# A two-layer attention trunk: k scaled by ScalarE in mixer B's prologue, later root steps, other steps for the weight splits, k stacks placed inside the v products, and a reordered start

## The chip, the cores and the metric

The kernel runs on one core of a Trainium2 chip. The metric is the device time of one execution in microseconds (us); the median of several runs is given. Engines are called as in the profile: PE (TensorE), DVE (VectorE), ACT (ScalarE), POOL (GpSimd), SP (SyncE, which here only issues DMAs). PE, DVE, ACT and POOL each carry out their own instructions in the order of the program and meet through semaphores; an instruction that waits holds up all that stand behind it on its engine.

## The reference

1024 tokens of width 1024 go through two layers. Layer 0 uses mixer A, neighbourhood attention over a 16 x 64 token grid: each query sees 8 x 16 keys around it, with a learned bias. Layer 1 uses mixer B, attention with 16 query heads and 4 key/value heads of 64; q and k are normalised per head and rotated by their grid position:

```python
proj = h @ w_in
q, k, v, gate = jnp.split(proj, [MIX_WIDTH, MIX_WIDTH + kv_w, MIX_WIDTH + 2 * kv_w], axis=-1)
q = rms_norm(q..., q_norm_g); k = rms_norm(k..., k_norm_g)
q = _apply_axial_rope(q, tabs); k = _apply_axial_rope(k, tabs)
sc = jnp.einsum('bkgqd,bksd->bkgqs', qb, k) * scale
pr = jax.nn.softmax(sc, axis=-1)
o = jnp.einsum('bkgqs,bksd->bkgqd', pr, v)
return (o * jax.nn.silu(gate)) @ w_out
```

Ahead of each mixer stands an RMS norm over the 1024 columns, behind it a residual sum and a gated projection of a per-layer embedding (in the kernel `ple`, `pp`). A last RMS norm ends the trunk.

## The kernel before

**Products.** Each float32 product is made of three products in a rounded form (fp32r): high by high, high by low and low by high, where the low half of a value is what its rounding left. So every operand of PE exists twice, as `HTh` and `HTl` (the normed tokens, transposed), `wh` and `wl` (weights), `PTh` and `PTl` (transposed attention weights), `KA` and `KB` (keys). `mm` (L324) is one matmul, `split3` three. A high half is a copy on ACT (a PSUM or SBUF source, an fp32r target), a low half a subtraction, mostly on DVE.

**Weights.** The class `Weights` (`WQ`) keeps the order in which 128 x 1024 units of weights are used. `stage` loads a unit by SP's DMA (L216) into one of two `wstage` buffers; a unit's load can start when the unit two before it is split, so SP's queue waits there, with the DMAs behind it. `pump` splits the next loaded unit: the high half at once (ACT, L235), the low half (L240) at the next `settle`, on DVE in one operation of 1024 columns or on POOL in four of 256 (`WQ.low`). `gate` says whether `pump` may split: `False` no, `True` one split and then `False`, `None` always. `get` forces whatever the product at hand still lacks. A split unit's staging buffer is free after its low half.

**Order.** `pulse()` runs `WQ.pump` and `post.tick`; what was put off by `post.add(n, f)` runs n pulses later. `mix(att, dense)` interleaves two lists: it runs the items of `att` one by one, a pulse behind each, and dense items in between in proportion to their written costs.

**Start of mixer A** (L942 to L1047), an order written out by hand: for token tile t, `load` (SP), `square` and `root` (ACT), `newton` (DVE, from tile 3 on `newton_p` on POOL), `scale` (DVE L923, whole or by halves of 512 columns), `ht` (four transposes L506 by PE, `HTh` L507 by ACT, `HTl` L508 by DVE, per half). `vpart(t, a, b)` runs items a to b of tile t's v products; chunk i of them uses unit i of the weights `avv`, and for tiles 0 and 1 a chunk comes in three items, one for each kind of product (the last of a chunk's three may be the one with `wl`). `split()` forces one split, both halves. The first unit's low half is on DVE, the following on POOL.

**Mixer B** has a prologue and 128 steps. The prologue makes q, k, v of the first heads (`qkv_items`, products of 512 columns into the one `d` bank), and half of the second heads'. Behind each fourth token tile `finish_norm` takes the norms of four tiles, 24 values each row: in the prologue (`pro[0]`) Newton steps on DVE, then `scale_tile` (L1229 to L1232) multiplies k tiles (128 x 128, two heads) on DVE and q tiles (128 x 256, four heads) on POOL. Later it is a `power` on POOL (L1217), a root step `newton` of three DVE operations (L1220 to L1222), and the scalings on POOL one pulse apart; a norm of more than 16 values (the second heads' q and k, two such norms) has four pulses more between them. `k_stack(i, hf)` transposes four k tiles (PE L1271, into `psT`, a pool of two banks) and makes `KA` (ACT) and `KB` (DVE, with copies on POOL) from them. `k_stack(1, ...)` makes keys that are first used near step 62.

Step n of 0 to 127 treats one head, half and tile: `f_S` (scores, PE; the minimum, DVE L1371), `f_E` (exponential, ACT L1377), `f_T` (8 transposes, PE L1389, in two banks of `psT`; `PTh` ACT L1391, `PTl` DVE L1392), and at even n `f_AV`, the product with v over two steps, first all matmuls with `PTh`, then what stands in `turned` (q stacks, transposes by PE into `psT`), then all with `PTl`. A step takes about 4.2 us. Step n's items of `att` are `turn`, [`f_AV`], `f_T` and `f_E` in either order, `f_S` of step n + 2, each with a pulse. The dense items between them are the second heads' qkv products (g = 0), gates, q products (g = 1, 2), and at the end `pp` (g = 3). `scores` sets `WQ.gate` to `True` behind odd n and to `False` behind even n below 112, and to `None` from 112 on; `turn` sets a `True` that wasn't used to `False`. So weights are split at one place in odd steps, and freely at the end.

Of the kernel before, what the change touches and what calls it, by code (L numbers as in the profile page):

```python
# [15 lines left out]
AF = mybir.ActivationFunctionType  # L16
# [17 lines left out]
DG, DR, DQ, DY, NP = 1, 2, 2, 1, 8  # L34
# [10 lines left out]
KD, KS = 3, 4  # L45
# [118 lines left out]
def trunk(ctx, tc, x, wts, rpb, gains, hgains, mask, sides, rope, gain0, out):  # L164
    nc = tc.nc
    sync, act, dve, pool, pe = nc.sync, nc.scalar, nc.vector, nc.gpsimd, nc.tensor
# [99 lines left out]
    WQ = Weights()  # L266
# [54 lines left out]
    post = Later()  # L321
# [180 lines left out]
    def to_ht(pt, t, xn, cs=(0, 1)):  # L502
        for c in cs:
            ps = pt.tile([128, 4, 128], F32, name="t")
            for k in range(4):
                pe.transpose(ps[:, k], xn[:, (4 * c + k) * 128:(4 * c + k + 1) * 128], ident)  # L506
            act.activation(HTh[:, t, 4 * c:4 * c + 4], ps, AF.Copy)  # L507
            dve.tensor_tensor(HTl[:, t, 4 * c:4 * c + 4], ps, HTh[:, t, 4 * c:4 * c + 4], ALU.subtract)  # L508
# [183 lines left out]
    def mixer_a():  # L692
        jobs = weight_sums()
        with ExitStack() as es:
# [195 lines left out]
            def load(t):  # L890
                sync.dma_start(X[t], x[t])

            def square(t):
                act.activation(junk, X[t], AF.Square, accum_out=stat[:, 0, t:t + 1])
# [4 lines left out]
            def newton(t):  # L899
                ss, y, r = stat[:, 0, t:t + 1], stat[:, 1, t:t + 1], stat[:, 2, t:t + 1]  # L900
                h, w = wk[:, 8 + t:9 + t], wk[:, 16 + t:17 + t]
                dve.tensor_scalar(h, ss, -0.5 / D, -0.5 * EPS, op0=ALU.mult, op1=ALU.add)  # L902
                dve.reciprocal(y, wk[:, t:t + 1])
                dve.scalar_tensor_tensor(w, y, h, y, op0=ALU.mult, op1=ALU.mult)
                dve.scalar_tensor_tensor(r, w, 1.5, y, op0=ALU.add, op1=ALU.mult)
# [15 lines left out]
            def scale(t, n=1024, cs=None):  # L921
                for c in cs or range(0, 1024, n):
                    dve.scalar_tensor_tensor(X[t][:, c:c + n], X[t][:, c:c + n], stat[:, 2, t:t + 1], gain[:, c:c + n],  # L923
                                             op0=ALU.mult, op1=ALU.mult)

            def ht(t, cs=(0, 1)):
                to_ht(psT, t, X[t], cs)
# [5 lines left out]
            def split():  # L933
                WQ.pump(True)
                WQ.settle()
# [21 lines left out]
            def vpart(t, a, b):  # L957
                for f in vs[t][a:b]:
                    f()
# [22 lines left out]
            root(2)  # L982
            scale(1, 512, (512,))
            newton(2)
            for t in range(5, NT - 1):
                load(t)
            X.append(ini.tile([128, D], F32, name="X", bufs=NT - 1))
            load(NT - 1)
            vpart(1, 0, 3)
            ht(1, (1,))  # L990
            scale(2, 512, (0,))
            vpart(1, 3, 5)
            vpart(0, 5, 6)
            vpart(1, 5, 6)
            ht(2, (0,))
            scale(2, 512, (512,))
            square(3)
            newton_p(3)
            split()
            vpart(2, 0, 1)  # L1000
            ht(2, (1,))
            split()
# [81 lines left out]
            for h in range(NH):  # L1084
                att = []
                for j in range(NT):
                    n = h * NT + j
# [28 lines left out]
                dense = []  # L1116
# [15 lines left out]
    def mixer_b(pend):  # L1132
        with ExitStack() as es:
# [30 lines left out]
            turned = []  # L1164
# [35 lines left out]
            def finish_norm(ss, tiles):  # L1200
                wk = sb.tile([128, 96], F32, name="wk", bufs=1)
                n = ss.shape[1]
                if pro[0]:
                    ops = [lambda: dve.tensor_scalar(ss, ss, 0.5 / HD, 0.5 * EPS, op0=ALU.mult, op1=ALU.add)]
                    ops += rsqrt_ops(ss, ss, wk)
                    for i in range(2):
                        post.add(1 + i, lambda i=i: [f() for f in ops[6 * i:6 * i + 6]])
                    for raw, rs in tiles:
                        post.add(2, lambda raw=raw, rs=rs: scale_tile(raw, rs, dve if rs.shape[1] == 2 else pool))
                    return  # L1210
                y, a = wk[:, 0:n], wk[:, n:2 * n]

                def power():
                    dve.tensor_scalar(ss, ss, 4.0 / HD, 4.0 * EPS, op0=ALU.mult, op1=ALU.add)
                    for c in range(0, n, 8):
                        w = slice(c, min(c + 8, n))
                        pool.tensor_tensor(y[:, w], ss[:, w], mhalf[:, :w.stop - c], ALU.pow)  # L1217

                def newton():
                    dve.tensor_tensor(a, y, y, ALU.mult)  # L1220
                    dve.scalar_tensor_tensor(a, a, -1.0, ss, op0=ALU.mult, op1=ALU.mult)
                    dve.scalar_tensor_tensor(ss, a, 3.0, y, op0=ALU.add, op1=ALU.mult)  # L1222
                post.add(DR, power)
                at = DR + NP + (4 if n > 16 else 0)
                post.add(at - 1, newton)
                for i, (raw, rs) in enumerate(tiles):
                    post.add(at + i, lambda raw=raw, rs=rs: scale_tile(raw, rs))

            def scale_tile(raw, rs, eng=pool):  # L1229
                nh = rs.shape[1]  # L1230
                r3 = raw.rearrange("p (h d) -> p h d", h=nh)
                eng.tensor_tensor(r3, r3, rs[:, :, None].to_broadcast([128, nh, 64]), ALU.mult)  # L1232

            def q_items(g, eng):
# [181 lines left out]
            def gates(p):  # L1416
                return [i for hf in range(2) for i in gate_items("bg", p, hf, dalloc, sb, gg)]

            def stacks(i):
                return [(lambda hf=hf: k_stack(i, hf), 450.0) for hf in range(2)]  # L1420
            first, second = qkv_items(0, dve, 4), qkv_items(1, pool, 2)
            ks, gf = stacks(0), gates(0)
# [13 lines left out]
            def exps(n):  # L1436
                def f():
                    f_E(*steps[n])
                f.first = True
                return f  # L1440

            def blocks(n):
                def f():
                    f_T(*steps[n])
                f.kind = "apart" if n % 2 else "blocks"
                return f
            for g in range(4):
                att = []
                for n in range(32 * g, 32 * g + 32):
                    h, hf, t = steps[n]  # L1450
                    av = n >= 2 and n % 2 == 0
                    w = CB if av else CN
                    def turn():
                        if WQ.gate:
                            WQ.gate = False
                        later.tick()
                    att.append((turn, w[0]))
                    if av:
                        att.append((lambda n=n: f_AV(*steps[n - 1]), w[1]))
                    te = [(blocks(n), w[2])]  # L1460
                    if n + 1 < len(steps):
                        te.append((exps(n + 1), w[3]))
                    if n % 2 == 0 and n > 0:
                        te.reverse()
                    att += te
                    if n + 2 < len(steps):
                        def scores(n=n):
                            f_S(*steps[n + 2])
                            WQ.gate = n % 2 == 1 if n < 112 else None
                        att.append((scores, w[4]))  # L1470
                    m = n + QS_AT
                    if m % 8 == 0 and m < len(steps):
                        hn, fn, _ = steps[m]
                        att.append((lambda hn=hn, fn=fn: turned.append(lambda: q_stack(hn // 2, fn)), 0.0))
                    if YLOAD_B <= n < YLOAD_B + NT:
                        att.append((lambda t=n - YLOAD_B: load_y(1, t), 0.0))
                if g == 3:
                    def last():
                        end[0] = 1
                        f_AV(*steps[-1])  # L1480
                    att.append((last, CB[1]))
                dense = []
                if g == 0:
                    gd = gates(1)
                    n = len(gd) // 2
                    dense += second[10:16] + gd[:n] + second[16:] + gd[n:]
                elif g == 3:
                    WQ.cap[3] = 2
                    dense += gates(6) + gates(7) + pp_items(1, dalloc, sb, TAGS_B)
                else:  # L1490
                    gd = gates(2 * g)
                    n = len(gd) // 2
                    qi = q_items(g + 1, pool)
                    ks = stacks(1) if g == 1 else []
                    dense += gd[:n] + ks[:1] + gd[n:] + qi[:KS] + ks[1:] + qi[KS:8] + gates(2 * g + 1) + qi[8:]
                mix(att, dense, hold=HOLD + 1 if g == 3 else 0)
            post.flush()
            later.flush()
# [466 lines left out]
```

## Time and profile before

| | us |
|---|---|
| median of 3 runs | 1500.2 (1499.02 to 1501.57) |
| the profiled execution | 1498.04 |
| its span, first to last instruction | 1496.3 |
| mean granted TensorE clock | 0.999 |
| DMA moved | 157.61 MB, 105 GB/s on the mean |

| from to (us) | part | PE busy |
|---|---|---|
| 0 to 50 | start of mixer A | 45.76 of 50 |
| 700 to 760 | prologue of mixer B | 58.48 of 60 |
| 760 to 890 | mixer B, first steps | 129.21 of 130 |
| 890 to 975 | steps with the moved parts | 80.53 of 85 |
| 975 to 1190 | | 215.00 of 215 |
| 1190 to 1320 | last steps of mixer B | 127.50 of 130 |

Lines of the timeline read: start, duration, engine, line of the program, operation, output tile and input tiles, shape, count (rows of the same kind that follow each other are joined, the duration is then from the first start to the last end), and in brackets how long the engine was idle before and whose end released it ("issue": nothing that the profile shows). Matmuls overlap in PE's pipe, so a matmul's duration is longer than the distance to the next start.

### The profile page before, as it was taken

Reading aid. Unit: us, or ns where it says so; the run is one execution under the profiler, and the core shown is the slowest. Engines: PE = TensorE matmul, PEld = TensorE weight load, DVE = VectorE, ACT = ScalarE, POOL = GpSimd, SP = SyncE. Lnnn points to the kernel's source line nnn. Section 1 sums busy time; section 2 is a strip of 40 time slices with the busy share of each in tenths; the row PEclk is TensorE's granted clock in tenths of the full one; section 3 lists DMA queues with packets and bytes.
Section 4 is the critical chain, followed back from the end, with each engine's and each line's share of the span. In section 5 each row is a group of like instructions: output and inputs, shape, how many; then the busy total and the mean of one; then the engine's idle time right before and its main releaser. Section 6 shows DMA issues by size and latency. Waiting matters only on the chain.

```text
span 1496.3 us, 23431 instructions
## 1 busy us (share of the span) xinstructions
PE 1473.0 (98%) x8305; PEld 1271.4 (85%) x8305; DVE 1057.6 (71%) x1922; ACT 910.5 (61%) x1820; POOL 469.0 (31%) x651
## 2 busy tenths in 40 slices
PE   8999999999999999999999999999999999999997
PEld 6888888988988887888878887889999988888886
DVE  4467776477477598757766787777877777789845
ACT  5477766477377535433456776767767777745432
POOL 3246775387265200020154352323140400000000
PEclk9999999999999999999999999999999999999999
DMA  6424574283132963262220111101101121763223
GB/s 225 134 89 152 108 164 138 65 171 97 36 89 85 332 245 99 93 207 85 71 71 12 40 51 45 35 23 42 59 28 44 57 64 64 247 238 107 79 97 128
DMA packets 91460, 157.61 MB, mean 105 GB/s; under 512 B 18256, under 2 KB 54352, under 8 KB 90832
## 3 DMA queue, kind: packets, MB, share of 16 engines
q1 hardware_dynamic: 87344, 143.80, 29.0%
q0 software_dynamic: 2560, 8.39, 3.9%
q10 hardware_dynamic: 1440, 3.94, 0.8%
q8 instruction: 66, 1.08, 0.3%
q14 instruction: 50, 0.41, 0.1%
HBM read 125.56 MB, written 50.83 MB: 118 GB/s over the span
## 4 chain that ended last, share of the span: by engine, by line
PE 53%; DVE 5%; ACT 2%; issue 1%; DMA 0%; POOL 0%; DVEq 0%; ACTq 0%; POOLq 0%
PE d L324 27%; PE s L324 9%; PE o L324 8%; PE t L1389 7%; PE t L506 1%; DVE PTl L1392 1%; PE t L324 1%; DVE wl L240 1%; ACT PTh L1391 0%; DVE mn L1371 0%; PE t L1341 0%; DVE xn L1742 0%; ACT wh L235 0%; DVE X L1631 0%; DVE QS L1351 0%
## 5 line engine op out<-in xcount | busy, mean ns | idle before, releaser
L324 PE MATMUL d<-wh,HTh 128*128 128x512 f32 (+1 forms) x800 | 285.3, 358 | 1.2 <-ACT wh L235 0.8
L324 PE MATMUL d<-wl,HTh 128*128 128x512 f32 (+1 forms) x800 | 281.9, 354 | 1.7 <-POOL wl L240 0.9
L324 PE MATMUL d<-wh,HTl 128*128 128x512 f32 (+1 forms) x800 | 282.4, 355 | 0.0
L1392 DVE TENSOR_TENSOR PTl<-t,PTh 128x512 fp32r<-128x512 f32 x256 | 164.6, 684 | 115.2 <-ACT PTh L1391 114.7
L324 PE MATMUL d<-HTh,wh 128*128 128x512 f32 x480 | 193.9, 404 | 0.0
L324 PE MATMUL d<-HTh,wl 128*128 128x512 f32 x480 | 188.7, 393 | 0.0
L324 PE MATMUL d<-HTl,wh 128*128 128x512 f32 x480 | 188.1, 392 | 0.0
L1377 ACT ACTIVATE P<-s,mn 128x1024 f32<-128x1024 f32 x128 | 142.9, 1116 | 48.6 <-DVE mn L1371 46.5
L324 PEld LDWEIGHTS d<-wl,HTh 128*128 128x128 f32 x800 | 150.9, 189 | 24.6 <-DVE wl L240 1.5
L324 PEld LDWEIGHTS d<-wh,HTh 128*128 128x128 f32 x800 | 150.5, 189 | 23.5 <-ACT wh L235 1.2
L324 PEld LDWEIGHTS d<-wh,HTl 128*128 128x128 f32 x800 | 150.8, 189 | 22.0 <-DVE wki L902 0.3
L1391 ACT ACTIVATE PTh<-t 128x512 fp32r<-128x512 f32 x256 | 138.7, 593 | 43.5 <-PE t L1389 42.3
L1371 DVE TENSOR_REDUCE mn<-s 128x1 f32<-128x1024 f32 x128 | 154.9, 1210 | 5.3 <-PE s L324 4.9
L1389 PE MATMUL t<-ident,P 128*128 128x128 f32 x1024 | 133.9, 273 | 4.1 <-DVE PTl L1392 4.0
L849 POOL TENSOR_TENSOR PTh<-PTh,SIDE 128x256 fp32r<-128x256 f32 x96 | 83.7, 872 | 169.8 <-ACT PTh L844 169.8
L324 PE MATMUL s<-KA,QS 128*128 128x512 f32 (+2 forms) x384 | 134.9, 405 | 0.0
L1389 PEld LDWEIGHTS t<-ident,P 128*128 128x128 f32 x1024 | 116.5, 141 | 14.8 <-DVE PTl L1392 7.2
L324 PE MATMUL o<-PTl,V 128*128 128x256 f32 (+2 forms) x672 | 120.5, 290 | 1.1 <-DVE PTl L1392 0.7
L324 PE MATMUL s<-KB,QS 128*128 128x512 f32 (+2 forms) x384 | 121.4, 370 | 0.0
L324 PE MATMUL o<-PTh,V 128*128 128x256 f32 (+2 forms) x672 | 118.6, 287 | 2.4 <-ACT PTh L1391 0.9
L240 DVE TENSOR_TENSOR wl<-wstage,wh 128x1024 fp32r<-128x1024 f32 x75 | 94.3, 1260 | 31.3 <-ACT wh L235 31.2
L324 PEld LDWEIGHTS o<-PTh,V 128*128 128x128 f32 x672 | 98.4, 190 | 11.3 <-ACT PTh L1391 4.4
(286 smaller groups left out, 2933.9 us busy)
## 6 DMA issues: line engine op xcount, KB each, us to landing
wstage<-in_wts SPq DMA_DIRECT2D x88, 512.0 KB
pp<-ppD SPq DMA_DIRECT2D x32, 256.0 KB
X<-in_x SPq DMA_DIRECT2D x15, 512.0 KB
rb<-rD SPq DMA_DIRECT2D x58, 128.0 KB
ppD<-th SPq DMA_DIRECT2D x20, 256.0 KB
tD0t<-in_wts SPq DMA_DIRECT2D x16, 256.0 KB
tD1t<-in_wts SPq DMA_DIRECT2D x16, 256.0 KB
xD<-X SPq DMA_DIRECT2D x8, 512.0 KB
```

What stands on the lines that cost most here:

```text
L240: eng.tensor_tensor(lo[:, c:c + n], s[:, c:c + n], hi[:, c:c + n], ALU.subtract)
L324: pe.matmul(ps, a, b, start=first, stop=last, skip_group_check=True)
L506: pe.transpose(ps[:, k], xn[:, (4 * c + k) * 128:(4 * c + k + 1) * 128], ident)
L849: pool.tensor_tensor(pt[:, 3 * j - 1:3 * j + 4:4], pt[:, f1:f1 + 1].to_broadcast([128, 2, 128]), SIDE[:, :2], ALU.mult)
L1371: dve.tensor_reduce(mn, ps, axis=AX.X, op=ALU.min)
L1377: act.activation(p, ps, AF.Exp, bias=mn, scale=-1.0, accum_out=RS[h, hf][:, t:t + 1])
L1389: pe.transpose(ps[:, i], p[:, k * 128:(k + 1) * 128], ident)
L1391: act.activation(PTh[:, ks, c], ps, AF.Copy)
L1392: dve.tensor_tensor(PTl[:, ks, c], ps, PTh[:, ks, c], ALU.subtract)
```

## The change

Five edits.

- In the start of mixer A, `scale(2, 512, (0,))` comes right behind `newton(2)`. Behind `vpart(1, 3, 5)` comes the split of unit 2, its low half on DVE in one operation; `ht(2, (0,))` and the scaling of tile 2's other half follow, ahead of `vpart(0, 5, 6)` and `vpart(1, 5, 6)`. The split that stood ahead of `vpart(2, 0, 1)` is gone.
- In mixer B's prologue k tiles are scaled by ACT, two activations of 128 x 64 with a scale from SBUF for each tile, instead of one DVE operation of 128 x 128: 8 DVE operations become 16 on ACT, in two batches of four tiles.
- The root step and the scalings of norms with more than 16 values come four pulses later.
- `WQ.gate` stays `False` behind steps with n % 8 = 5, and the rule of the odd steps holds to the end (n < 126) instead of to 111.
- `k_stack(1, 0)` and `k_stack(1, 1)` leave the dense list. They are put into `turned` behind steps 37 and 41 and run inside the v products of steps 38 and 42. Two items of `att` with cost 0 are added (two more pulses), and the dense list is 900 shorter in cost.

```diff
             newton(2)
+            scale(2, 512, (0,))
             for t in range(5, NT - 1):
                 load(t)
...
             ht(1, (1,))
-            scale(2, 512, (0,))
             vpart(1, 3, 5)
+            WQ.low = dve
+            split()
+            WQ.low = pool
+            ht(2, (0,))
+            scale(2, 512, (512,))
             vpart(0, 5, 6)
             vpart(1, 5, 6)
-            ht(2, (0,))
-            scale(2, 512, (512,))
             square(3)
             newton_p(3)
-            split()
             vpart(2, 0, 1)
...
-                        post.add(2, lambda raw=raw, rs=rs: scale_tile(raw, rs, dve if rs.shape[1] == 2 else pool))
+                        post.add(2, lambda raw=raw, rs=rs: scale_tile(raw, rs, act if rs.shape[1] == 2 else pool))
...
-                at = DR + NP + (4 if n > 16 else 0)
+                at = DR + NP + (8 if n > 16 else 0)
...
+                if eng is act:
+                    for i in range(nh):
+                        act.activation(r3[:, i], r3[:, i], AF.Copy, scale=rs[:, i:i + 1])
+                    return
                 eng.tensor_tensor(r3, r3, rs[:, :, None].to_broadcast([128, nh, 64]), ALU.mult)
...
-                            WQ.gate = n % 2 == 1 if n < 112 else None
+                            WQ.gate = n % 2 == 1 and n % 8 != 5 if n < 126 else None
                         att.append((scores, w[4]))
+                    if n in (37, 41):
+                        att.append((lambda n=n: turned.append(lambda: k_stack(1, n // 41)), 0.0))
...
-                    ks = stacks(1) if g == 1 else []
-                    dense += gd[:n] + ks[:1] + gd[n:] + qi[:KS] + ks[1:] + qi[KS:8] + gates(2 * g + 1) + qi[8:]
+                    dense += gd + qi[:8] + gates(2 * g + 1) + qi[8:]
```

## The prediction

> **What bounds the kernel now.** I read the page's first part, then the PE waits over mixer B, then the timeline around every place where PE waited and an edited line stood near. The page:
>
> ```profile
> span 1496.3 us, 23431 instructions
> PE 1473.0 (98%) x8305; PEld 1271.4 (85%) x8305; DVE 1057.6 (71%) x1922; ACT 910.5 (61%) x1820; POOL 469.0 (31%) x651
> ```
>
> PE has next to no idle time on average, so a change that leaves its matmuls alone can only win back its waits. The waits of PE from 690 to 1320 us, grouped (us, times, longest):
>
> ```profile
> PE t L1389 <- DVE PTl L1392: 4.0, 4, 2.8
> PE t L1271 <- DVE PTl L1392: 1.2, 2, 0.9
> ```
>
> The two largest groups, 5.2 us in six waits, both end with PTl, DVE's low half of the attention weights. One PTl is short (1.27 for two, in a row below), so a wait of 2.8 has a queue behind it: what stood ahead of PTl on DVE. That is what the edits move. Each place is costed by itself, since a PE that has a microsecond more or less hands it on to the end.
>
> A wait costs more than its idle time. Four matmuls of 512 columns take 1.08 in the row at 16.05 below and one alone takes 0.39 (751.77, below), so they start (1.08 − 0.39)/3 = 0.23 apart; after a wait the row before has run out its 0.39 instead of 0.23, and 0.16 goes as well. I add 0.16 to each direct wait.
>
> **Prologue A.** The timeline from 1 to 25 us (start, duration, engine; behind `<-` what ended the idle time):
>
> ```profile
> 1.64 0.43 SPq L216 DMA_DIRECT2D wstage<-in_wts  x1
> ...
> 7.43 1.06 ACT L235 ACTIVATE wh<-wstage 128x1024 fp32r<-128x1024 f32 x1 [1.42 <-DMA wstage<-in_wts]
> ...
> 9.77 0.33 SPq L216 DMA_DIRECT2D wstage<-in_wts  x1
> ...
> 15.95 0.69 DVE L508 TENSOR_TENSOR HTl<-t,HTh 128x512 fp32r<-128x512 f32 x1 [0.81 <-ACT HTh L507]
> 16.05 1.08 PE L324 MATMUL d<-wl,HTh 128*128 128x512 f32 x4
> 16.55 0.74 DVE L923 SCALAR_TENSOR_TENSOR X<-X,stat,gain 128x512 f32<-128x512 f32 x1
> ...
> 18.71 0.50 PE L324 MATMUL s<-wh,HTh 128*128 128x512 f32 x1 [0.69 <-ACT HTh L507]
> ...
> 19.44 0.50 PE L324 MATMUL s<-wh,HTl 128*128 128x512 f32 x1
> ...
> 19.59 1.05 ACT L235 ACTIVATE wh<-wstage 128x1024 fp32r<-128x1024 f32 x1
> ...
> 21.65 3.52 POOL L240 TENSOR_TENSOR wl<-wstage,wh 128x256 fp32r<-128x256 f32 x5
> ...
> 24.53 0.50 PE L324 MATMUL d<-wl,HTh 128*128 128x512 f32 x1 [0.88 <-POOL wl L240]
> ```
>
> PE waits for tile 2 (its scaling ends at 17.29, a microsecond after PE was ready for its transposes but for the four matmuls at 16.05), then 0.69 for its HTh, and 0.88 for unit 2's low half, which POOL makes in four pieces. New order: scale(2, low) fits before HTl at 15.95, where DVE idled 0.81. Behind vpart(1,3,5) ACT does unit 2's high half from about 15.95 if the unit is there. It is issued at 9.77; the first unit, issued at 1.64, was in use 5.8 later, which puts this one at 15.6 (an estimate). So: high half, 1.05, to 17.0, HTh of tile 2, about 0.6, to 17.6; DVE low half, 1.22 (the row at 753.44, below), from 17.0 to 18.2, HTl, 0.69, to 18.9, scale(2, high), 0.74, to 19.7. PE: transposes at 16.05, the four matmuls to 17.8, vpart(2,0,1) then, with a wait of about 0.7 for HTl: its third matmul starts at 19.0 instead of 19.44, 0.45 earlier, and 0.88 + 0.16 is saved at 24.53: **1.5**. Bounds: 0, if the unit lands 1.5 later and ACT's queue holds HTh behind it; 1.9, the waits 0.69 and 0.88 with 0.16 each. SP's queue gains: its mask and bias loads stand behind the next unit's load, which waits for a staging buffer, and that comes free sooner.
>
> **k scaling by ACT.** The second batch of norms stands before the last qkv products; first a group by shape (busy, mean ns), then the timeline:
>
> ```profile
> L1314 ACT ACTIVATE V<-th 128x64 fp32r<-128x64 f32 x32 | 6.2, 240 | 0.0
> ```
> ```profile
> 747.16 0.63 ACT L626 ACTIVATE th<-G 128x512 f32<-128x512 f32 x1
> ...
> 748.98 0.18 DVE L343 SCALAR_TENSOR_TENSOR ss<-wk 128x24 f32<-128x24 f32 x1
> 749.20 2.16 DVE L1232 TENSOR_TENSOR qt<-qt,ss 128x128 f32<-128x128 f32 x4
> 749.31 2.52 POOL L1232 TENSOR_TENSOR qt<-qt,ss 128x256 f32<-128x256 f32 x4 [8.23 <-DVE ss L343]
> ...
> 751.28 1.64 DVE L240 TENSOR_TENSOR wl<-wstage,wh 128x1024 fp32r<-128x1024 f32 x1
> ...
> 751.77 0.39 PE L324 MATMUL d<-wh,HTh 128*128 128x512 f32 x1
> ...
> 753.44 1.22 DVE L240 TENSOR_TENSOR wl<-wstage,wh 128x1024 fp32r<-128x1024 f32 x1
> ...
> 756.15 1.06 ACT L235 ACTIVATE wh<-wstage 128x1024 fp32r<-128x1024 f32 x1 [2.92 <-DMA wstage<-in_wts]
> ...
> 757.26 0.50 PE L324 MATMUL d<-wh,HTh 128*128 128x512 f32 x1 [0.77 <-ACT wh L235]
> ...
> 758.51 0.50 PE L324 MATMUL d<-wl,HTh 128*128 128x512 f32 x1 [0.76 <-DVE wl L240]
> ```
>
> The k tiles hold DVE for 2.16; the low half behind them ends at 752.92, only then is its staging buffer free, the next unit's load takes until 756.15 (3.2), and PE waits 0.77 + 0.76. Those two waits, with 0.16 for each and what they drag along, are 1.97 of lost start-to-start time at most. After: DVE's low half runs from 749.2, beside POOL as at 751.28 (1.64), to 750.85; the load lands at 754.1; ACT's high half ends by 755.6 and the low half by 756.9, where PE wants them near 756.3 and 756.6. The second wait keeps some 0.3, the first goes.
>
> The price is on ACT. It has eight Copies of 128x64 with a scale from SBUF; the nearest row is V's Copy of the same shape, 0.24 each, so 8 × 0.25 = 2.0. Bounds: below, 1.9, that row itself; above, 8 × 0.63 = 5.0, the 128x512 row at 747.16. In the queue they stand ahead of ACT's next evacuation of PE's one d bank and wait there for ss (749.16): it starts near 751.85 where PE wants the bank at 751.77, 0.15 lost. At the upper price 3 us would be lost. Gain: **1.2**, from −3 to 1.97. The first batch, before PE's first steps of attention, delays an evacuation by 2 to 3 us; PE still has its other products then, so I cost it at nothing.
>
> Here the sum leans on DVE and POOL working side by side: 2.16 and 2.52 both lie within 749.20 to 751.83, a stretch of 2.63. [...]
>
> **Root steps and splits at step 29.** Timeline:
>
> ```profile
> 894.30 1.24 DVE L1220 TENSOR_TENSOR wk<-wk 128x24 f32<-128x24 f32 x1
> ...
> 899.18 1.53 DVE L240 TENSOR_TENSOR wl<-wstage,wh 128x1024 fp32r<-128x1024 f32 x1
> ...
> 900.63 1.09 DVE L611 TENSOR_TENSOR Y<-Y,rb 128x512 fp32r<-128x512 f32 x1
> ...
> 901.65 1.27 DVE L1392 TENSOR_TENSOR PTl<-t,PTh 128x512 fp32r<-128x512 f32 x2
> ...
> 902.38 1.25 PE L1389 MATMUL t<-ident,P 128*128 128x128 f32 x8 [2.81 <-DVE PTl L1392]
> ```
>
> The largest wait: PE's transposes need a psT bank that PTl empties, and DVE does the root step (1.24 and two of 0.18 as at 748.98, 1.6 with it), then the minimum that releases the exponential, then a low half, then Y, then PTl. Step 29 has n % 8 = 5, so the split goes to step 31; without 1.53, PTl's first half ends at 900.8 and PE, which wanted the bank at 902.38 − 2.81 − 0.16 = 899.4, still waits 1.4. The root step moved away brings the minimum, and with it the exponential and PTh behind it on ACT, about 1.6 forward. Four pulses later it stands after the minimum and ahead of PTl(30), now without POOL's products beside it, about 0.6: PTl's first half ends at 899.1, 0.3 before its time. Gain **2.9**, of 2.81 + 0.16. If the root step keeps its 1.6 and Y its 1.09, 1.2 is left of the wait: lower bound 1.8. Behind the moved root step POOL's eight scalings and the k stacks' input come about a step later, still steps ahead of the k stacks in step 38.
>
> **k stacks.** Timeline, the four places:
>
> ```profile
> 921.97 0.66 PE L1271 MATMUL t<-ident,qt 128*128 128x128 f32 x4 [0.88 <-DVE PTl L1392]
> ...
> 938.22 1.25 PE L1389 MATMUL t<-ident,P 128*128 128x128 f32 x8 [0.28 <-DVE PTl L1392]
> ...
> 957.45 0.66 PE L1271 MATMUL t<-ident,qt 128*128 128x128 f32 x4 [0.34 <-DVE PTl L1392]
> ...
> 968.17 1.34 PE L324 MATMUL o<-PTl,V 128*128 128x256 f32 x8 [0.16 <-DVE PTl L1392]
> ```
>
> Put among dense products, the transposes want a psT bank that PTl still holds, and later transposes feel it. Inside an AV, between its PTh and PTl products, the last step's banks have been read. Directly 0.88 + 0.34 + 2 × 0.16 = 1.54 goes; the other two (0.28 + 0.16 + 2 × 0.16 = 0.76) follow later in the same stretches. The bank is then taken ahead of the next step's transposes, as with the q stacks there already. I take **1.7** of 2.3; 1.0 as lower bound, if a stack in an AV meets the next transposes.
>
> **Steps 101 and 113.** Timeline:
>
> ```profile
> 1209.26 0.93 PE L1389 MATMUL t<-ident,P 128*128 128x128 f32 x5 [0.69 <-DVE PTl L1392]
> ...
> 1253.37 1.23 DVE L240 TENSOR_TENSOR wl<-wstage,wh 128x1024 fp32r<-128x1024 f32 x1
> ...
> 1255.25 0.98 PE L324 MATMUL o<-PTl,V 128*128 128x256 f32 x5 [0.58 <-DVE PTl L1392]
> ```
>
> In both a low half of 1.23 stands ahead of PTl. The first split moves from step 101 (n % 8 = 5) to 103: **0.8** (0.69 + 0.16 = 0.85 at most). The second ran since the gate was open from step 112; gated, it goes to an odd step: **0.7** (0.74 at most). Lower bound 0 for each, if the wait turns up where the split has gone; the others were made in odd steps without one. The last unit's split slips to the dense phase, long before its use. Fewer allowed steps make units later; one that isn't there when its product comes is split at once, with PE waiting for it: that belongs to the second rival.
>
> **Sum.** 1.5 + 1.2 + 2.9 + 1.7 + 0.8 + 0.7 = 8.8. The profiled execution, 1496.3 of span and 1.7 around it, took 1498.0, so it goes to 1489.2. The median of the runs, 1500.2, lies 2.2 above it; with the same distance the forecast is 1491.4.
>
> **The rivals.** *First: part two gives nothing.* If POOL's four q scalings (749.31 to 751.83) hold DVE's low half off, it ends at 751.83 + 1.22 = 753.05, no sooner than 752.92: the load and both waits stay. 8.8 − 1.2 = 7.6: 1492.6. For it: 1.64 beside POOL against 1.22 alone. Against: the stretch of 2.63 above. Chance 0.08.
>
> *Second: the waits return.* The moved root step stands ahead of PTl(30) with its full 1.6, and moved splits meet PTl in their new steps. Part three falls to 1.8, the last two and the stacks to half (0.75 and 1.0), the prologue keeps 0.5 and part two nothing: 4.0, so 1496.2. For it: every split of 1.23 stands before some PTl. Against: most of them cost no wait. Chance 0.16; some of that, gains under 3.0, is 0.07, with ACT's Copies near 0.6 among its causes.
>
> *Third: slower.* The granted clock falls as PE's last waits close. The windows view's row for 1190 to 1320 us (its columns: length, busy time and count of PE, PEld, DVE, ACT, POOL; clock, DMA share, GB/s):
>
> ```profile
> 1190.00:1320.00 130.00, 127.50 (x792) 111.22 (x790) 95.22 (x134) 95.38 (x168) 7.50 (x5) 1.00 0.37 123
> ```
>
> A clock lower by 1% costs 1% of 1473, 14.7: 1491.4 + 14.7 = 1506.1. It decides from 0.6%, 8.8/1473. Against: the clock is 1.00 with PE at 98% here (127.50 of 130), and 0.6% more, 8.8 of 1473, is all that is added. Chance 0.03.
>
> *Fourth: the change doesn't do what it says.* Had unit 2 not landed by 16, the split ahead of ht(2) would hold up tile 2: part one 0, 1492.9, within my own case.
>
> **How the numbers follow.** Forecast 0.73 (1489.5, all parts at their upper bounds, 10.7, to 1494.7: steps 101 and 113 at 0, the stacks and step 29 at their lower bounds), first rival 0.08, second 0.16, third 0.03. 0.2%, 3.0 us, is about what a measurement of this kernel can tell from no change. Faster by more, under 1497.2: 0.73 + 0.08 + 0.09 = 0.90, less 0.03 for prices that none of the rows show, 0.87; within: 0.10; slower: 0.03. The range, 1489.0 to 1497.0: below it more than 11 us would have to go, past the sum of the upper bounds, 0.04; above it, from the second and third rival, 0.13.
>
> **What would show it.** Right: no PE wait over 0.5 near 24 us, at 757, 902, 922, 1209 and 1255; PTl(30) ending its first half before PE's transposes; ACT Copies at L1232's successor near 0.25; the second qkv norms' Newton rows a step later; span near 1487.5. Wrong: an idle PE of over 1 us in 16 to 20 or in 749 to 753 with ACT named as its releaser (head of line), a wait for PTl in steps 31, 38, 42 or 103 as large as the old one, or a clock under 1.00.

## The result and the profile after

The changed kernel took 1492.02 us (median of five runs, 1490.53 to 1494.49), the kernel before 1500.85 in the five runs beside it (1499.02 to 1501.57): a ratio of 0.9947, 95% interval 0.9933 to 0.9962, about 8 us less by the ratio and 8.8 by the medians. The forecast was 1491.4. The profiled execution took 1492.02 with a span of 1490.2, 6.1 less than the span before. Its page:

```profile
span 1490.2 us, 23430 instructions
PE 1470.3 (99%) x8305; PEld 1270.7 (85%) x8305; DVE 1053.9 (71%) x1915; ACT 914.6 (61%) x1836; POOL 464.8 (31%) x647
```

The PE waits from 690 to 1320 us of the changed kernel, as in the prediction's second fence, the six largest groups (lines of the code moved down by six to seven):

```profile
PE t L1395 <- DVE PTl L1398: 1.3, 3, 0.7
PE o L324 <- ACT PTh L1397: 0.9, 3, 0.4
PE o L324 <- DVE Y L529: 0.9, 2, 0.5
PE d L324 <- ACT G L625: 0.8, 1, 0.8
PE d L324 <- DVE wl L240: 0.8, 1, 0.8
PE d L324 <- ACT th L656: 0.5, 1, 0.5
```

The transposes' waits for PTl fell from 4.0 to 1.3, and the k stacks' group (1.2) is gone. Two lines are new: PE waiting for ACT's G and for ACT's th. Both are costs of the change.

To see each place I summed, over all PE instructions of a stretch, what each start lay behind the usual distance to the start before it (0.229 for 512 columns, 0.120 for 256, 0.109 for a 128-column transpose). The times of the stretches are counted from each execution's own first instruction.

| stretch (us) | edit | before | after | won | forecast |
|---|---|---|---|---|---|
| 12.5 to 50 | start of mixer A | 3.27 | 1.51 | 1.8 | 1.5 |
| 738 to 765 | k scaling on ACT | 1.90 | 2.38 | −0.5 | 1.2 |
| 890 to 910 | root step, split of step 29 | 3.22 | 0.82 | 2.4 | 2.9 |
| 910 to 975 | k stacks | 3.16 | 0.15 | 3.0 | 1.7 |
| 1190 to 1230 | split of step 101 | 1.48 | 0.52 | 1.0 | 0.8 |
| 1230 to 1270 | split of step 113 | 1.60 | 0.65 | 0.9 | 0.7 |
| 1270 to 1325 | the next split | 2.19 | 3.52 | −1.3 | 0 |
| the rest | first loads, mixer A and others | | | −1.2 | 0 |

That makes 6.1, the difference of the spans, where the sum of the prediction was 8.8. Four terms were larger than reckoned, one was smaller, and the k scaling and the end of mixer B, with the rest, were negative. Of the rest, 0.5 lies before 12.5 us and 0.5 from 50 to 400 us, where nothing was edited.

The other twelve profiles, all of kernels that differ from these two in one edit or a few, go with the edits. With the old start the first stretch loses 3.3 to 3.4 (four profiles in all), with the new one 1.5 (eight; POOL's low half, below, less). With the k stacks at their old place the fourth loses 3.1 to 3.2 (three profiles), at the new one 0.1 to 0.2 (eleven). From 50 to 400 us, where no run has an edit, the same sum is anything from 2.5 to 6.0, so single times say less than stretches.

**The start** of the changed kernel, timeline:

```profile
16.28 1.05 ACT L235 ACTIVATE wh<-wstage 128x1024 fp32r<-128x1024 f32 x1
...
17.36 1.23 DVE L240 TENSOR_TENSOR wl<-wstage,wh 128x1024 fp32r<-128x1024 f32 x1 [0.25 <-ACT wh L235]
...
19.25 0.50 PE L324 MATMUL s<-wh,HTl 128*128 128x512 f32 x1 [0.64 <-DVE HTl L508]
```

Unit 2 was there when ACT came to it, and the low half, done at 18.6, has no wait behind it any more; PE's one wait, 0.64 for HTl behind the low half, is the 0.7 of the forecast.

**The k scaling.** Timeline of the changed kernel:

```profile
748.25 2.03 ACT L1236 ACTIVATE qt<-qt,ss 128x64 f32<-128x64 f32 x8 [5.08 <-DVE ss L343]
748.36 2.34 POOL L1238 TENSOR_TENSOR qt<-qt,ss 128x256 f32<-128x256 f32 x4 [8.23 <-DVE ss L343]
...
750.18 1.04 ACT L235 ACTIVATE wh<-wstage 128x1024 fp32r<-128x1024 f32 x1
...
751.13 0.57 ACT L625 ACTIVATE G<-d 128x512 f32<-128x512 f32 x1
751.25 1.23 DVE L240 TENSOR_TENSOR wl<-wstage,wh 128x1024 fp32r<-128x1024 f32 x1 [3.04 <-ACT wh L235]
...
751.75 0.50 PE L324 MATMUL d<-wh,HTh 128*128 128x512 f32 x1 [0.78 <-ACT G L625]
...
755.69 1.06 ACT L235 ACTIVATE wh<-wstage 128x1024 fp32r<-128x1024 f32 x1 [1.23 <-DMA wstage<-in_wts]
...
756.80 0.51 PE L324 MATMUL d<-wh,HTh 128*128 128x512 f32 x1 [0.19 <-ACT wh L235]
...
758.07 0.50 PE L324 MATMUL d<-wl,HTh 128*128 128x512 f32 x1 [0.75 <-DVE wl L240]
```

The eight Copies cost 2.03, as reckoned. But ACT stood idle for 5.08 ahead of them, waiting for ss, and behind them in its queue stand the high half and G. So DVE, freed of the k tiles, waits 3.04 for that high half, and its low half ends at 752.48; measured from ss (748.2) that is 4.3, against 3.8 before (749.2 to 752.92). The first batch, at 723.38 with 4.98 of idle time ahead of it, cost PE no wait, as reckoned.

**Step 29/30.** DVE and PE, timeline:

```profile
893.80 1.29 POOL L614 TENSOR_TENSOR Y<-Y,rb 128x512 f32<-128x512 f32 x1
...
893.99 1.65 DVE L1357 TENSOR_TENSOR QS<-th,QS 64x512 fp32r<-64x512 f32 x1
...
897.65 0.18 DVE L1222 TENSOR_TENSOR wk<-wk 128x24 f32<-128x24 f32 x1
...
898.80 1.28 DVE L1398 TENSOR_TENSOR PTl<-t,PTh 128x512 fp32r<-128x512 f32 x2
...
899.54 1.25 PE L1395 MATMUL t<-ident,P 128*128 128x128 f32 x8 [0.38 <-DVE PTl L1398]
```

The root step's first operation takes 0.18 at its new place, where it took 1.24 beside POOL's L614. QS, which took its old place, lasts 1.65 instead of 0.69: that price stayed.

**The end of mixer B**, ACT with the DMAs that it issues (ACTq), then PE:

```profile
1278.79 0.33 ACTq L290 DMA_DIRECT2D HTh<-yD1h  x1
...
1280.59 1.07 ACT L235 ACTIVATE wh<-wstage 128x1024 fp32r<-128x1024 f32 x1
1283.74 0.33 ACTq L290 DMA_DIRECT2D HTl<-yD1l  x1
1284.19 0.60 ACT L656 ACTIVATE th<-d 128x512 f32<-128x512 f32 x1 [2.53 <-DMA HTl<-yD1l]
```
```profile
1284.84 0.50 PE L324 MATMUL d<-wh,KA 128*128 128x512 f32 x1 [0.45 <-ACT th L656]
...
1287.15 1.04 PE L1395 MATMUL t<-ident,P 128*128 128x128 f32 x6 [0.65 <-DVE PTl L1398]
```

ACT issues the loads of y for tiles 0 to 3. Its sequencer was ahead of the engine here, whose work went on to 1281.66; at the last of the loads the sequencer stood from 1279.1 to 1283.74, and the engine was idle for 2.53 with th behind it. The trace names the semaphore that an issue waits for and the one that its landing raises; for these four issues of ACT, in both kernels, the two are the same, so an issue stands until the DMA that used its semaphore before has landed. In the changed kernel that is the HTl load of tile 2 (semaphore 110, issued at 1277.99, landed at 1283.72, the next issue at 1283.74), in the kernel before the HTh load of tile 2 (semaphore 107, issued at 1285.08 of that execution, landed at 1289.01, the next issue at 1289.03). SP's and ACT's DMAs draw on the same semaphores (in the changed kernel from 1277.62 on: ACT 107 and 110, SP 108, ACT 106), so the weight load and the split that the gate moved could shift them; the runs below with the gate open show that the gate edit is the cause, that it works by this shift is argued.

### The profile page after: what moved, and what is told of

Same layout as the page of the kernel before. It is cut to its first block, busy times and chain, and to the rows that moved or that the text cites. A ratio compares the mean times of both kernels' runs of the same rounds, so it can differ in the third digit from the quotient of the medians.

```text
span 1490.2 us, 23430 instructions
## 1 busy us (share of the span) xinstructions
PE 1470.3 (99%) x8305; PEld 1270.7 (85%) x8305; DVE 1053.9 (71%) x1915; ACT 914.6 (61%) x1836; POOL 464.8 (31%) x647
## 3 DMA queue, kind: packets, MB, share of 16 engines
q8 instruction: 66, 1.08, 0.3%
## 4 chain that ended last, share of the span: by engine, by line
PE 55%; DVE 4%; ACT 2%; issue 1%; DMA 1%; POOL 0%; ACTq 0%; POOLq 0%; DVEq 0%
PE d L324 27%; PE s L324 10%; PE o L324 8%; PE t L1395 7%; PE t L506 1%; PE t L324 1%; PE t L1347 0%; DVE PTl L1398 0%; DMA HTl<-yD1l 0%; DVE xn L1749 0%; ACT wh L235 0%; DVE X L1638 0%; DVE wl L240 0%; DVE mn L1377 0%; DVE wl L1536 0%
```

## The experiments

Each is compared with the same places of the two kernels; the first eleven are single executions with a profile, whose times are given but not built on, since nine runs of the kernel before lie up to 5.5 apart. L numbers are those of each kernel.

**k tiles back on DVE** (the changed kernel):

```diff
-post.add(2, ... scale_tile(raw, rs, act if rs.shape[1] == 2 else pool))
+post.add(2, ... scale_tile(raw, rs, dve if rs.shape[1] == 2 else pool))
```

> The changed kernel with the k tiles scaled by DVE again, as before; the other four edits stay. Theory: ACT's eight Copies hold up its own queue, a high half of weights and the evacuation of the d bank, so that PE's wait of 0.78 at 751.75 is their price; with DVE doing the work that wait goes and the wait for wh, now 0.19 at 756.80, comes back to 0.77, the wait for wl stays 0.75. Sum of the PE waits from 745 to 760: 1.5 instead of 1.7. Rival (the edit gains its 1.2 and the wait at 751.75 has another cause): 0.78 stays and the two others are 1.5, sum 2.3. The median can't tell these apart.

1490.29. The two waits of this stretch, PE's timeline:

```profile
755.42 0.49 PE L324 MATMUL d<-wh,HTh 128*128 128x512 f32 x1 [0.89 <-ACT wh L235]
...
756.68 0.50 PE L324 MATMUL d<-wl,HTh 128*128 128x512 f32 x1 [0.77 <-DVE wl L240]
```

The wait for G is gone, the one for wh is back: 1.66 instead of 1.72 of waits, and 2.01 of lost time from 738 to 765 instead of 2.38. In the five other kernels with the scaling on ACT the stretch lost 2.48 to 2.93. The edit gained nothing and cost about half a microsecond.

**One pulse later on DVE.**

```diff
+post.add(3 if rs.shape[1] == 2 else 2, ... scale_tile(raw, rs, dve if rs.shape[1] == 2 else pool))
```

> The changed kernel with the k tiles scaled by DVE one pulse later than before, so that a low half of weights stands ahead of them. Theory (what matters is only how soon the low half near 751 frees its staging buffer): the low half ends near 750.4 instead of 752.5, the next unit lands near 753.6 instead of 755.7, and PE's waits at 751.75 and 756.80 both go; the wait for wl at 758.07 falls from 0.75 to under 0.3, so 1.4 to 1.9 is won over the changed kernel. Rival (the load is limited by other things than its buffer, or the k tiles are wanted sooner): the wait for wh stays near 0.2 to 0.8 or PE waits for the k tiles at its transposes near 754.6.

1494.14, a miss: waits of 0.88 and 0.76 as in the run above. The low half is emitted at the pulse behind that of its high half, so the k tiles still stood ahead of it (752.37 after 750.29); the idea wasn't tried by this run. The next one with it was the run with four pulses, below.

**The gate alone, the root step alone** (the kernel before with one edit each):

```diff
-WQ.gate = n % 2 == 1 if n < 112 else None
+WQ.gate = n % 2 == 1 and n % 8 != 5 if n < 112 else None
```
```diff
-at = DR + NP + (4 if n > 16 else 0)
+at = DR + NP + (8 if n > 16 else 0)
```

> The kernel before with one thing changed: no weight split in steps with n % 8 = 5 (free from step 112 on, as before). The root step stays where it was. By the prediction's working 1.4 of the 2.81 at step 29 stays and the wait at step 101 (0.69) goes: 1.5 and 0.7 won. Rival: the split is all of it at step 29 (nothing of the wait stays, 2.8 won), or the wait moves to step 31 or 103 in full.

> The kernel before with one thing changed: the root step and the scalings of the norms with more than 16 values four pulses later. By the prediction's working the root step leaves 1.6 of time ahead of PTl of step 30 and takes 0.6 back: the wait at step 29 falls from 2.81 to about 1.8. Rival, after the changed kernel's trace (there the QS operation that takes the place of the root step's first operation lasts 1.65 instead of 0.69, beside the same POOL operation): what the root step paid for was POOL, and the next operation pays it now, so the wait falls by 0.2 at most, to 2.6.

1497.39 and 1497.86. PE's wait at step 29/30, first with the gate, then with the root step:

```profile
902.27 1.25 PE L1389 MATMUL t<-ident,P 128*128 128x128 f32 x8 [1.25 <-DVE PTl L1392]
```
```profile
902.11 1.25 PE L1389 MATMUL t<-ident,P 128*128 128x128 f32 x8 [1.52 <-DVE PTl L1392]
```

So 2.81 falls to 1.25 without the split (forecast 1.4) and to 1.52 without the root step (forecast 1.8; the rival's 2.6 fell). Neither alone is enough: 1.56 and 1.29 add up to 2.85, and both together won 2.43. With the gate alone the wait at step 101 went too, and none came at 103; from 1190 to 1230 0.92 is lost instead of 1.48. DVE's queue with the root step moved shows where its 1.29 comes from:

```profile
895.42 1.66 DVE L1351 TENSOR_TENSOR QS<-th,QS 64x512 fp32r<-64x512 f32 x1
...
898.37 0.69 DVE L1351 TENSOR_TENSOR QS<-th,QS 64x512 fp32r<-64x512 f32 x1
899.09 1.22 DVE L240 TENSOR_TENSOR wl<-wstage,wh 128x1024 fp32r<-128x1024 f32 x1
900.23 0.18 DVE L1220 TENSOR_TENSOR wk<-wk 128x24 f32<-128x24 f32 x1
...
900.77 0.69 DVE L611 TENSOR_TENSOR Y<-Y,rb 128x512 fp32r<-128x512 f32 x1
```

Before, the second QS took 1.17, the low half 1.53 and Y 1.09, beside POOL's eight scalings, which the root step releases. Now POOL works later and they take 0.69, 1.22 and 0.69: 1.19 less. The root step itself, 1.6 before and 0.6 now, is worth no more than what QS gives back (1.0 against 0.97).

**The k stacks alone** (the kernel before):

```diff
+if n in (37, 41):
+    att.append((lambda n=n: turned.append(lambda: k_stack(1, n // 41)), 0.0))
...
-ks = stacks(1) if g == 1 else []
-dense += gd[:n] + ks[:1] + gd[n:] + qi[:KS] + ks[1:] + qi[KS:8] + gates(2 * g + 1) + qi[8:]
+dense += gd + qi[:8] + gates(2 * g + 1) + qi[8:]
```

> The kernel before with one thing changed: the two k stacks inside the v products of steps 38 and 42 instead of among the dense items. Theory: the four waits of 0.88, 0.28, 0.34 and 0.16 between 920 and 970 go and none comes near steps 38 and 42; with 0.16 for each wait that is 2.3 won. Rival (part of it comes back as a wait for the next transposes or from the shifted dense items): 1.0 to 1.7 won, with new waits for PTl in steps 38, 42 or later. The wait of 2.81 at step 29 stays in both.

1497.40. From 905 to 975 PE has no wait that the waits view names; lost time from 910 to 975 is 0.17 instead of 3.16. The stretch from 765 to 890 and those behind 975 are as before, so nothing came back. In this execution something else shows behind the wait of 2.82 at step 29/30; windows view:

```profile
900.00:904.00 4.00, 1.18 (x8) 0.65 (x7) 4.00 (x5) 2.27 (x6) 2.99 (x3) 1.00 0.34 85
904.00:908.00 4.00, 4.00 (x14) 3.22 (x13) 3.77 (x5) 2.35 (x5) 0.00 (x0) 0.57 0.56 177
```

The granted clock (third number from the right) is 0.57 for four microseconds; the matmuls of 512 columns start 0.427 apart there against the usual 0.229, about half speed, and 1.5 more is lost. More of it in the last section.

**Tile 3's loads issued by SP** (the changed kernel):

```diff
-(act if t < 4 and l else sync).dma_start(...)
+(act if t < 3 and l else sync).dma_start(...)
```

> The changed kernel with the loads of y for token tile 3 of layer 1 issued by SP instead of ACT. In the changed kernel ACT stood still from 1281.66 to 1284.19 while a DMA issue in its queue waited for the landing of an earlier one. Theory: that wait is the whole cause of the new PE waits of 0.45 and 0.65 near 1285 and 1287; with the issue on SP's queue both go, 1.4 won. Rival (the weight split that the new gate put ahead of ACT's evacuation in step 121 is the cause): waits of 0.4 or more stay at both places.

1491.02. The two waits at 1285 and 1287 went, but a wait for th of 0.41 came at 1292, behind a copy of ACT out of PSUM that waited 1.74 for the landing of a store `ppD<-th`, and the wait of 0.54 near 1298 became one of 0.90. The stretch lost 3.26 instead of 3.52, 0.3 won where 1.4 was expected. So the standstill at 1284 came from the issue in ACT's queue, and taking it out of there won next to nothing; why the store landed late wasn't followed.

**The gate open from 112 on, and from 116 on** (the changed kernel):

```diff
-WQ.gate = n % 2 == 1 and n % 8 != 5 if n < 126 else None
+WQ.gate = n % 2 == 1 and n % 8 != 5 if n < 112 else None
```

(and `n < 116` in the second).

> The changed kernel with the gate open from step 112 on, as before, and closed in steps with n % 8 = 5 below. Theory: the PE wait of 0.58 for PTl in step 113 comes back and the two waits near 1285 and 1287 (0.45, 0.65) go, since the DMAs are dealt out as before; with 0.16 for each wait that is 0.74 lost and 1.4 won, 0.7 faster than the changed kernel. Rival (the waits near 1285 belong to another edit): they stay, and it is 0.7 slower.

> The changed kernel with the gate rule of the odd steps up to n < 116 and open from there, instead of n < 126. Theory: the split that cost 0.58 in step 113 keeps its harmless place, and the next one goes back to step 120, ahead of the loads of token tile 3 in ACT's queue, which then wait for the same semaphores as before the change: the waits of 0.45 and 0.65 near 1285 and 1287 go, 1.0 to 1.4 won. Rival: ACT's standstill comes back with any split near the loads; then at least 0.6 stays there.

1492.25 and 1490.93. With 112 the wait of 0.58 in step 113 is back (1230 to 1270: 1.60) and the two at 1285 are gone (1270 to 1325: 2.13): that stretch belongs to the gate edit. With 116 both are gone. PE's waits from 1270 to 1320 with 116, all there are:

```profile
PE o L324 <- DVE Y L529: 0.5, 1, 0.5
PE o L324 <- ACT PTh L1397: 0.3, 1, 0.3
```

1.4 less is lost there than in the changed kernel, with 0.64 from 1230 to 1270.

**Unit 2's low half on POOL** (the changed kernel):

```diff
-WQ.low = dve
 split()
-WQ.low = pool
 ht(2, (0,))
```

> The changed kernel with unit 2's low half, in the start of mixer A, made by POOL in four pieces again, at the new place of the split. Theory (the split's new place is what counts): ACT's high half from about 16.3, POOL's low half ends near 20.2, ahead of its use near 23, DVE is free for HTl 1.2 earlier, so PE's wait of 0.64 at 19.25 goes too and the start gets 0.6 to 0.8 shorter. Rival (DVE was needed): PE waits for wl again near 23, 0.5 or more. The first loads land up to 1 us apart from run to run, so distances from the first product are compared, not times.

1492.12. Timeline of the start:

```profile
17.20 2.82 POOL L240 TENSOR_TENSOR wl<-wstage,wh 128x256 fp32r<-128x256 f32 x4 [2.26 <-ACT wh L235]
...
17.65 0.69 DVE L508 TENSOR_TENSOR HTl<-t,HTh 128x512 fp32r<-128x512 f32 x1 [0.74 <-ACT HTh L507]
...
18.39 0.50 PE L324 MATMUL s<-wh,HTl 128*128 128x512 f32 x1
```

Measured from the first product (9.29 here, 9.48 in the changed kernel), HTl is done 0.7 earlier, PE has no wait there, and POOL's 2.82 end at 20.0, ahead of the first use near 23. 0.95 is lost from 12.5 to 50 instead of 1.51. What counted was the place of the split; DVE wasn't needed.

**The k tiles behind the low half** (the changed kernel, DVE, the second batch four pulses behind its norms).

```diff
+wait = 2 + 2 * len(batch)
+batch.append(1)
 for raw, rs in tiles:
-    post.add(2, ... act if rs.shape[1] == 2 else pool)
+    post.add(wait if rs.shape[1] == 2 else 2, ... dve if rs.shape[1] == 2 else pool)
```

> The changed kernel with the k tiles scaled by DVE, the second batch four pulses behind its norms instead of two, which puts the four operations behind the low half of the weights in DVE's order (with one pulse they still stood ahead of it). Theory: the low half starts with ss, as ACT's high half is done by then, and ends 2.2 sooner than with the k tiles ahead of it; the staging buffer's next load lands 2.2 to 2.5 sooner than in the run with one pulse, and the waits for wh (0.88) and for wl (0.76) both go: 1.9 won against scaling ahead, 1.7 to 2.1 against the changed kernel between 745 and 765. Rival (POOL's four q scalings hold the low half off, or the load doesn't follow its buffer): waits of 0.5 or more stay at both.

1491.80. Timeline:

```profile
750.17 1.23 DVE L240 TENSOR_TENSOR wl<-wstage,wh 128x1024 fp32r<-128x1024 f32 x1
750.39 3.35 POOL L1243 TENSOR_TENSOR qt<-qt,ss 128x256 f32<-128x256 f32 x4 [8.32 <-DVE ss L343]
751.32 2.57 DVE L1243 TENSOR_TENSOR qt<-qt,ss 128x128 f32<-128x128 f32 x4
...
754.74 1.06 ACT L235 ACTIVATE wh<-wstage 128x1024 fp32r<-128x1024 f32 x1 [0.53 <-DMA wstage<-in_wts]
...
762.00 0.50 PE L324 MATMUL s<-KA,QS 128*128 128x512 f32 x1 [0.21 <-POOL KA L1296]
...
763.21 0.50 PE L324 MATMUL s<-KB,QS 128*128 128x512 f32 x1 [0.48 <-POOL KB L1297]
```

Both waits for the weights went: the next unit's high half starts 4.6 behind ss (750.17), where it took 7.0 before (749.2 to 756.15). In their place stand two shorter ones for POOL's copies of KA and KB, 0.69 together, near 762. Lost time from 738 to 765: 1.07, 1.3 less than in the changed kernel, short of the 1.7 to 2.1 expected, and 0.8 less than in the kernel before.

**The root step six pulses later** (the changed kernel):

```diff
-at = DR + NP + (8 if n > 16 else 0)
+at = DR + NP + (10 if n > 16 else 0)
```

> The changed kernel with the root step of the large norms six pulses later than before, instead of four. Theory: it then stands behind PTl of step 30 in DVE's order, its 0.6 leaves the way of that PTl, and the last 0.38 of the wait at step 29/30 goes (0.5 won with 0.16 for the wait). Rival (the QS operation beside POOL, 1.65, is what delays PTl): 0.2 or more stays.

1491.20. The wait of 0.38 became 0.30; more than 0.2 stayed, as the rival had it. DVE's queue shows that PTl no longer waits for DVE at all:

```profile
897.77 0.69 DVE L611 TENSOR_TENSOR Y<-Y,rb 128x512 fp32r<-128x512 f32 x1
898.84 1.29 DVE L1398 TENSOR_TENSOR PTl<-t,PTh 128x512 fp32r<-128x512 f32 x2 [0.38 <-ACT PTh L1397]
```

With the root step out of the way DVE stands idle for 0.38 until ACT's PTh is there, so the root step's last 0.6 bought next to nothing. PTh stands behind the exponential (897.11 to 898.2), the exponential waits for the minimum (895.79 to 897.0), and the minimum stands behind QS on DVE (894.11 to 895.76, 1.65). That the 0.30 is the price of QS beside POOL is read from this chain; no run moved QS or POOL's product.

**The four mends together**: the diffs of the runs with POOL's low half, the k tiles behind the low half, `n < 116` and the root step six pulses later, in one kernel.

> The changed kernel with four mends together: unit 2's low half on POOL, the k tiles on DVE behind the low half, the gate rule to n < 116, the root step six pulses later than before. Theory: the gains of the single runs add, 0.55 + 1.9 + 1.2 + 0.5 = 4.1 off the changed kernel's 1492.0, so 1487.9, a ratio of 0.991 to 0.992 to the kernel before; the sum of lost start-to-start time of PE from 738 to 765 falls under 0.7 and from 1230 to 1325 under 2.9. Rival (a wait that is taken away only gives its time to the next one): under 2 in all, 1490 or more.

1487.02 (median of five runs, 1486.85 to 1491.02) against 1499.97 before (nine runs): ratio 0.991, interval 0.9896 to 0.9923, which lies wholly below the changed kernel's interval. That is 5.0 less than the changed kernel's median, where 4.1 was expected. Lost time in the seven stretches of the table is 0.83, 0.88, 0.74, 0.14, 0.50, 1.06 and 2.15, 6.3 instead of 9.55, so the trace shows 3.25 of the 5.0. The profiled execution is the slowest of the five (1491.02) and has a half-speed stretch in mixer A, where no edit is: from 200 to 400 us it loses 4.6, the changed kernel's 2.1. The wait for KB (0.48) keeps the second above the 0.7 expected, and a wait of 0.18 for ACT's L1352 at 1258 is new, so the end of mixer B lost 3.2 instead of under 2.9.

## Why the prediction was right, and where not

The time was right, the sum behind it only in part, and some of the hit was luck. The sum of 8.8 was to bring the profiled span to 1487.5, and it came to 1490.2. The forecast then added 2.2, by which the profiled execution before lay under its median; the profiled execution after is its median, so that distance fell away. The sum promised 2.7 more than the traces show, and the 2.2 took most of it back.

- **Start of mixer A: right**, 1.8 against 1.5, by the row that was named (the wait at 24.53) and with the wait of 0.7 that was reckoned.
- **k scaling by ACT: wrong in sign**, −0.5 against 1.2, though within its bounds. The Copies' price (2.0) was right. What failed is "After: DVE's low half runs from 749.2": I took ACT's high half, which ran at 747.70 before, to stay ahead of the Copies. It stands behind them in the program, and ACT has nothing to do for 5.08 while it waits for ss, with that high half and G in the queue: a new wait of 0.78 for G, and of the two old ones 0.19 and 0.75, where 0 and 0.3 were reckoned. The first rival had the time nearly right (1492.6) by another mechanism, POOL holding DVE off. The stretch of 2.63 that was set against that rival doesn't speak against it: within it DVE and POOL took turns (last section). What speaks against it is the run with the k tiles behind the low half, where the low half starts first and takes 1.23.
- **Step 29: right in kind, 0.5 too high**. The split's share came out as worked out (1.25 left against 1.4). By its own terms PTl's first half was to end at 900.8 − 1.6 + 0.6 = 899.8, not at the 899.1 that was written; PE wanted it at 899.4, and 0.38 of the wait stayed. The root step's share was mis-sized in its parts: the 1.6 was mostly the price of working beside POOL, which the next operation paid in its stead, and the gain came from POOL's scalings going later.
- **k stacks: 3.0 against 1.7**, above my bound of 2.3. All four waits went, and with them 0.7 of smaller delays that no wait row shows.
- **Step 101 and step 113: right**, 1.0 and 0.9 against 0.8 and 0.7.
- **What was not in the sum**: "the last unit's split slips to the dense phase" was costed at nothing, and the split between, from step 120 to 121, wasn't looked at. With it came ACT's standstill, 0.4 to 1.3 in the changed kernel and the runs with the same gate and loads (2.63 to 3.52 against 2.19). I had followed the split on DVE and PE, and not the DMA issues beside it in ACT's queue.
- **The rivals.** Waits that return, the second, came in part, with 1.3 lost at the end of mixer B. The slower one (a falling clock) did not come: the mean granted clock is 0.999 in both profiles.

The spans of the two profiled executions differ by 6.1 and the medians by 8.8. The profiled execution before was faster than its two medians by 2.2 and 2.8, so some 2.7 of the medians' difference stands in no row of the two traces. The mean granted clock of nine runs of before was 0.996 to 0.998, of the five runs after 0.997 to 0.999; 0.001 of 1490 is 1.5 us. That fits the half-speed stretches below, of which waits that are taken away leave fewer; it is argued, not shown.

## What to carry to other kernels

Moving work to an idle engine pays only if nothing behind it in that engine's queue is wanted sooner than its input: here eight Copies of 0.25 made their queue wait 5.08 us for their norms, and putting the old DVE work behind one weight split won 0.8 where the move lost 0.5. When an instruction that issues DMAs or splits weights is moved, follow every queue that it leaves and joins, and the landings that the DMA issues in them wait for (ACT's 2.53 at 1284.19). The wait of PE at step 29/30 that two works caused together, 2.81, went only with both out of the way (1.25 and 1.52 left with one of them gone, 0.38 with both), so cost such works together.

## What the runs showed of the hardware

**Half-speed stretches after PE waits.** Between 50 and 1480 us PE ran for some 3.4 us at about half speed (in the run with the k stacks alone its matmuls of 512 columns start 0.427 apart until 907.85, against 0.229, and the granted clock of 0.57 on the mean of 4 us is 3.4 us at the 0.50 that the changed kernel shows from 1487 to 1490) in five of the fourteen profiles, six times in all. Each time it began within two microseconds of the end of a wait or of a pair of waits, 1.6 to 2.8 in all: behind step 29/30, behind the pair at 757 (twice), and behind a pair in mixer A at 315 (three times). Each cost 1.4 to 1.7. The waits at step 29/30 and at 757 had none in other executions; a wait of 1.73 in mixer A came in these three alone. So these waits of 1.6 to 2.8 cost, beside their idle time, 1.4 to 1.7 more. What decides whether a stretch follows stays open.

**DVE and POOL took turns.** The timeline joins rows; taken one by one, those of the kernel before from 749.20 to 751.83 end in turn: DVE 749.49, POOL 749.96, DVE 750.11, POOL 750.58, DVE 750.73, POOL 751.21, DVE 751.35, POOL 751.83. POOL's end lies 0.47 to 0.48 behind DVE's, DVE's 0.14 or 0.15 behind POOL's, though alone they take 0.61 and 0.29. The low half that stood behind them (751.28, 1.64) ends 1.08 behind POOL's last. In the run with the k tiles behind it the low half starts first, takes its 1.23 and ends at 751.40, and POOL's first scaling ends 0.47 after that; first that scaling, then one of the changed kernel with DVE idle:

```profile
750.39 1.48 POOL L1243 TENSOR_TENSOR qt<-qt,ss 128x256 f32<-128x256 f32 x1 [8.32 <-DVE ss L343]
```
```profile
748.36 0.61 POOL L1238 TENSOR_TENSOR qt<-qt,ss 128x256 f32<-128x256 f32 x1 [8.23 <-DVE ss L343]
```

So in these rows the later one of two waits for the earlier one, and only some 0.14 of it (0.61 less 0.47, 0.29 less 0.15, 1.23 less 1.08) passes during the wait. The same holds for the rows near step 29: the root step's 1.24, which takes 0.18 alone, ends 0.04 behind POOL's L614 (895.50).
